# Attention of a two-layer trunk: stacked scores and a late block of heads, replaced by 64-row scores and heads spread over the projections

## The chip, the cores and the metric

The kernel runs on one core of a Trainium2 chip. The metric is the time of one execution on the device in microseconds, the median of several runs. The engines are named TensorE (PE; its weight loads are PEld), VectorE (DVE), ScalarE (ACT), GpSimd (POOL) and SyncE (SP, which here only issues DMAs).

## What is computed

A decoder trunk of two layers on one sequence of 256 tokens and 1024 features in float32. Layer 0 mixes tokens with attention, layer 1 with a matrix memory (mLSTM); a SwiGLU feed-forward network follows each, and a norm ends the trunk. The change touches layer 0's attention. With 256 tokens there is one key block of 256, so what remains of the block-sparse attention is plain causal softmax attention of 16 heads of 64:

```python
qkv = jnp.einsum('bsd,de->bse', xn, w_qkv).reshape(B, S, 3, ATTN_HEADS, ATTN_HEAD_DIM)
q = partial_rotary(qkv[0], cos, sin)
k = partial_rotary(qkv[1], cos, sin)
...
s_own = jnp.einsum('bhqd,bhkd->bhqk', qc, k_own, preferred_element_type=jnp.float32)
s_own = jnp.where(kpos[None, :] <= qpos[:, None], s_own, -jnp.inf)
p = jax.nn.softmax(jnp.concatenate([s_sel, s_own], axis=-1), axis=-1)
...
return jnp.einsum('bsd,de->bse', o, w_o)
```

## The kernel before

Activations lie transposed, features on partitions and tokens along a row. Every operand of a large matmul is split into a high and a low part (`xh`, `xl`, `wh`, `wl`; written `fp32r`), and `mm3` (L188) adds the three products high x high, high x low and low x high. Weights come as *units* of 128 x 1024 in the order of `unit_names` (L45): SP loads a unit into `raw` (L141), ScalarE casts it to `wh` (L159), VectorE subtracts for `wl` (L150). `prefetch` keeps four units of lead.

The attention stage runs in this order. `first_block` (L258) makes q and k of head pairs 0 to 3 in four PSUM banks, one unit per step of the contraction. Then a `Stream` (L293) walks through the rest: a generator per block of projections yields after every six matmuls of 256 columns (or three of 512), which is one *position*; work on heads hangs in a queue at positions, and a step that is not ready is tried again half a position later. The instructions of TensorE, VectorE and ScalarE keep the order in which they are recorded this way; GpSimd's and SP's come out of the scheduler. `ORDER` makes the stream v of heads 0 to 7, then q and k of pairs 4, 5, 6, part of v of heads 8 to 15, pair 7, the rest of v. Behind these come the output projection (`out_start`, `out_steps`) and `finish` (L375), then the feed-forward network.

A pair of heads goes through `rotary` (L480: a shuffle and a product on VectorE, a product and a sum on GpSimd), then `stacks` (L441): q and k are split into `u` (ScalarE cast L445, VectorE subtraction L449) and six DMAs (L452 to L454) put the parts of each head on top of each other in `stk`, so that one 128-row matmul does two of the three products:

```python
def dots(o, T, a0, na, m0, nm):
    a = T[:, 256 + a0:256 + a0 + na]
    mm(o, a, T[:, m0:m0 + nm], True, False)
    mm(o, a, T[:, 512 + m0:512 + m0 + nm], False, True)
```

A head then takes `scores` (L517), `softmax` (VectorE, L529), `exps` (ScalarE, L535), `recip`, `normalize` (ScalarE, L545), `transposes` (L555), the split of the transposed probabilities (`ph` on ScalarE L561, `pl` on VectorE L566) and `values` (L572). The heads start at position 26, one every 3 positions. v is kept as `VT` with the high and the low part of a head side by side in 128 columns, so the values of a head come out as two sums in 128 partitions; `heads_out` (ScalarE copy L591), `out_sum` (VectorE L597), `out_split` (L603) and `out_low` (L607) add the two, put two heads together and split the result for the output projection.

Of the kernel before, what the change touches and what calls it, by code (L numbers as in the profile page):

```python
# [24 lines left out]
ORDER = (0, 4, 5, 6, 1, 7, 1)  # L25
V1 = 4
# [18 lines left out]
def unit_names():  # L45
# [7 lines left out]
    def a_units():  # L53
        n, v = [], each("av", range(4))
        parts = {0: [v[0:4]], 1: [v[4:4 + V1 // 4], v[4 + V1 // 4:]]}
        for i in ORDER:
            n += parts[i].pop(0) if i < 4 else each("aqk", [i])
        return n

# [10 lines left out]
    n = outer("aqk") + a_units() + each("ao", range(4)) + ffn(0)  # L70
# [6 lines left out]
def trunk_kernel(ctx: ExitStack, tc: tile.TileContext, x, w, wg, fw, tab, out):  # L77
# [180 lines left out]
    def first_block(name, n, hooks={}):  # L258
# [164 lines left out]
    banks = first_block("aqk", n)  # L423
# [43 lines left out]
    with ExitStack() as actx:  # L467
# [10 lines left out]
        st = {}  # L478

        def rotary(hp, bank):  # L480
            b3 = bank.rearrange("p (g t) -> p g t", g=2)
            qk = ap.tile([P, 512], F32, name="qk", tag="qk", bufs=2)
# [12 lines left out]
        stacked = set()  # L495

        def v_evict(n0, banks, part=0):

            for t in range(2):
                dst = VT[:, t, n0 * 8:n0 * 8 + 8].rearrange("p (h two) d -> p h (two d)", two=2)  # L500
                hi = dst.rearrange("p h (c d) -> p h c d", d=64)[:, :, 0::3]
                src = banks[t].rearrange("p (h two d) -> p h two d", two=2, d=64)
                if part == 0:
                    nc.scalar.activation(hi, src, AF.Copy, scale=n.r[:, t:t + 1])
                    continue
                for o in range(2):
                    nc.vector.scalar_tensor_tensor(out=dst[:, :, 64 + o * 64:128 + o * 64], in0=src[:, :, o],  # L507
# [511 lines left out]
```

## Time and profile before

| what | value |
|---|---|
| median of 3 runs | 608.32 us (605.78 to 609.12) |
| profiled execution | 605.8 us |
| its span, first to last instruction | 604.0 us |
| mean granted TensorE clock | 0.996 |
| TensorE busy | 590.7 us (98%), 4524 matmuls |
| VectorE busy | 415.8 us (69%) |
| ScalarE busy | 340.9 us (56%) |
| GpSimd busy | 77.9 us (13%) |
| chain that ended last | PE 83%, DVE 5%, ACT 4%, DMA 3% |

Times in the profile count from the span's start. A timeline row has the start, the duration, the engine, the line, the operation, the tile it writes and those it reads, the size of the stationary tile, the size of the moving one, and in brackets the idle time before it with the engine whose work ended it. Matmuls overlap in the pipeline: what one costs is the distance between two starts, not its duration. A row of the chain has the start, the duration and the work that the end of the span hung on at that time. Names with a trailing `x48` stand for so many instructions.

### The profile page before, as it was taken

What the parts mean: (1) busy time and instruction counts of PE and PEld (TensorE: products, weight loads), DVE (VectorE), ACT (ScalarE), POOL (GpSimd) and SP (SyncE); (2) the same over time, 40 slices, a digit from 0 to 9 for tenths busy, and PEclk for the clock granted to TensorE, in tenths of its full rate; (3) what the DMA queues carried; (4) which work ended last, traced back from release to release, by engine and by line L of the source; (5) the groups of instructions that cost most, each with busy time, mean ns of one, the idle gap of its engine ahead of it and who ended that gap; (6) DMA issues with size and microseconds to landing.
All of it is one profiled execution on the core that took longest, in us unless ns stands there. A gap on an engine that the chain in (4) does not pass through costs nothing.

```text
span 604.0 us, 11573 instructions
## 1 busy us (share of the span) xinstructions
PE 590.7 (98%) x4524; PEld 561.2 (93%) x4524; DVE 415.8 (69%) x663; ACT 340.9 (56%) x611; POOL 77.9 (13%) x81
## 2 busy tenths in 40 slices
PE   8997999999999999999999999999999999999995
PEld 7987998999999999999999878999999999999984
DVE  5899898797866666566388678858776656556532
ACT  7645999767544444445275478846754444444412
POOL 2574320042000000000031300114100000000000
PEclk9999999999999999999999999999999999999999
DMA  8778965358655656555428868343955555565401
GB/s 312 286 216 260 263 200 159 140 180 305 214 196 189 207 179 206 183 201 190 163 81 302 255 218 222 110 141 117 308 175 200 178 187 197 175 194 190 141 0 69
DMA packets 36342, 116.39 MB, mean 193 GB/s; under 512 B 4544, under 2 KB 7360, under 8 KB 36288
## 3 DMA queue, kind: packets, MB, share of 16 engines
q1 hardware_dynamic: 36288, 115.66, 58.7%
q8 instruction: 35, 0.57, 0.4%
q14 instruction: 19, 0.16, 0.1%
HBM read 105.15 MB, written 1.05 MB: 176 GB/s over the span
## 4 chain that ended last, share of the span: by engine, by line
PE 83%; DVE 5%; ACT 4%; DMA 3%; issue 2%; SPq 1%; POOL 1%; POOLq 0%; ACTq 0%; DVEq 0%
PE ps L186 46%; PE acc L186 36%; DMA raw<-w 2%; DVE wl L150 2%; DMA stk<-u 1%; ACT wh L159 1%; ACT p L535 1%; ACT p L545 1%; DVE xl L207 1%; DVE u L449 1%; DVE VT L507 0%; PE ps L555 0%; SPq L452 0%; POOL sh L487 0%; POOL qk L488 0%
## 5 line engine op out<-in xcount | busy, mean ns | idle before, releaser
L150 DVE TENSOR_TENSOR wl<-raw,wh 128x1024 fp32r<-128x1024 f32 (+2 forms) x199 | 244.1, 1233 | 109.5 <-ACT wh L159 106.9
L159 ACT CAST wh<-raw 128x1024 fp32r<-128x1024 f32 (+2 forms) x199 | 205.5, 1038 | 184.9 <-PE ps L186 102.7
L186 PE MATMUL ps<-xh,wh 128*128 128x256 f32 x864 | 242.4, 281 | 0.8 <-ACT wh L159 0.8
L186 PE MATMUL ps<-xh,wl 128*128 128x256 f32 x864 | 241.0, 279 | 0.5 <-DVE wl L150 0.5
L186 PE MATMUL ps<-xl,wh 128*128 128x256 f32 x864 | 240.7, 279 | 0.0
L186 PEld LDWEIGHTS ps<-xh,wh 128*128 128x128 f32 x864 | 163.0, 189 | 2.1 <-ACT wh L159 1.2
L186 PEld LDWEIGHTS ps<-xh,wl 128*128 128x128 f32 x864 | 163.7, 189 | 1.1 <-DVE wl L150 1.1
L186 PEld LDWEIGHTS ps<-xl,wh 128*128 128x128 f32 x864 | 163.0, 189 | 0.7
L186 PE MATMUL acc<-hh,wh 128*128 128x256 f32 x176 | 48.6, 276 | 0.0
L186 PE MATMUL acc<-hl,wh 128*128 128x256 f32 x176 | 48.6, 276 | 0.0
L186 PE MATMUL acc<-hh,wl 128*128 128x256 f32 x176 | 48.6, 276 | 0.0
L219 POOL TENSOR_TENSOR ssum<-ssum,sq 128x512 f32<-128x512 f32 x12 | 20.5, 1708 | 198.6 <-issue 163.7
L644 DVE TENSOR_TENSOR tgu<-ps,R 128x512 f32<-128x512 f32 x42 | 28.6, 690 | 20.9 <-PE ps L186 20.9
L186 PE MATMUL acc<-wh,xh 128*128 128x512 f32 x96 | 39.0, 406 | 0.0
L186 PE MATMUL acc<-wh,xl 128*128 128x512 f32 x96 | 37.8, 393 | 0.0
L186 PE MATMUL acc<-wl,xh 128*128 128x512 f32 x96 | 37.7, 392 | 0.0
L186 PE MATMUL acc<-wh,hh 128*128 128x512 f32 x88 | 34.7, 394 | 0.0
L186 PE MATMUL acc<-wl,hh 128*128 128x512 f32 x88 | 34.7, 394 | 0.0
L186 PE MATMUL acc<-wh,hl 128*128 128x512 f32 x88 | 34.3, 390 | 0.0
L186 PEld LDWEIGHTS acc<-hl,wh 128*128 128x128 f32 x176 | 33.0, 188 | 0.0
L186 PEld LDWEIGHTS acc<-hh,wl 128*128 128x128 f32 x176 | 33.0, 188 | 0.0
L186 PEld LDWEIGHTS acc<-hh,wh 128*128 128x128 f32 x176 | 33.0, 188 | 0.0
(180 smaller groups left out, 853.8 us busy)
## 6 DMA issues: line engine op xcount, KB each, us to landing
raw<-w SPq DMA_DIRECT2D x195, 512.0 KB, 4.2
stk<-u SPq DMA_DIRECT2D x24, 192.0 KB, 4.3
stk<-u SPq DMA_DIRECT2D x24, 128.0 KB, 4.2
stk<-u SPq DMA_DIRECT2D x24, 64.0 KB, 3.6
out<-yout SPq DMA_DIRECT2D x4, 256.0 KB, 2.2
XV<-x SPq DMA_DIRECT2D x7, 128.0 KB, 6.2
tab_t<-tab SPq DMA_DIRECT2D x1, 708.0 KB, 6.9
fwb<-fw SPq DMA_DIRECT2D x1, 512.0 KB, 3.5
```

The source lines that it names most:

```text
L150: nc.vector.tensor_sub(wl[:, sl], raws[c][:, sl], wh[:, sl].bitcast(F32))
L159: nc.scalar.copy(wh[:, sl], raws[c][:, sl])
L186: nc.tensor.matmul(o, lhsT=lhsT, rhs=rhs, start=start, stop=stop, skip_group_check=True)
L207: nc.vector.scalar_tensor_tensor(out=self.l[:, f], in0=X[:, f], scalar=wc, in1=self.h[:, f].bitcast(F32), op0=ALU.mult, op1=ALU.subtract)
L219: nc.gpsimd.tensor_add(self.ssum, self.ssum, sq)
L449: nc.vector.tensor_sub(u[:, 512:1024], mv, u[:, 0:512].bitcast(F32))
L535: nc.scalar.activation(pt[:, sl], pt[:, sl], AF.Exp, bias=mx[:, t:t + 1], scale=-1.0, accum_out=ss[:, t:t + 1])
L545: nc.scalar.activation(pt[:, sl], pt[:, sl], AF.Copy, scale=ss[:, t:t + 1])
L644: nc.vector.tensor_mul(t.rearrange("p (g t) -> p g t", g=2), bank.rearrange("p (g t) -> p g t", g=2), n.R2())
```

## The change

- `first_block` of the attention (unit name `aqkv*`) makes q and k of pairs 0 and 1 and, in the two other banks, v of heads 0 to 7; the stream then makes q and k of pair 2, half of v of heads 8 to 15, pair 3, the other half, pairs 4 to 7. The number and the size of the units stay.
- `rotary` no longer leads to `stacks`. `split_qk` makes `u` (cast, and 1.5 positions later the subtraction), and `scores` multiplies straight from it: for each of two heads three products over the head's own 64 rows, the heads in turns, each into its own PSUM bank.
- Each pair of heads has a start of its own (`A_PAIR`), from position 9 to 73; its transposes follow 6 and 7 positions later, its values 12.
- `VT` keeps a head's high part in 64 columns and its low part in the next 64. `values` adds three products per half of the keys into 64 partitions, the two heads of a pair side by side along the row, so the sum of two halves is gone: `high_o` casts and `low_o` subtracts straight from PSUM.
- Buffers: `qk` 3, `u` 3, `p` 4, `ph` and `pl` 4, `oh` and `ol` 8.

```diff
-A_D1, A_X, A_D2, A_N, A_D3, A_L, A_D4, A_O1, A_O2 = 0.5, 1, 3, 1, 1, 1.5, 0.5, 1, 1
-A_O3, A_D5, A_D6, A_E, A_R, A_S, A_S2, A_W = 1, 2, 0, 1, 5, 6, 1.5, 1
-A_START, A_STEP, A_T, A_V = 26, 3.0, 8, 14
+A_PAIR = (9, 18, 27, 36, 48, 57, 65, 73)
+A_U, A_T, A_V, A_W = -4, 6, 12, 1
...
-    n = outer("aqk") + a_units() + each("ao", range(4)) + ffn(0)
+    n = outer("aqkv") + each("aqk", [2]) + each("av", [2]) + each("aqk", [3]) + each("av", [3])
+    n += each("aqk", range(4, 8)) + each("ao", range(4)) + ffn(0)
...
-            for i in range(4):
+            for i in range(pairs):
...
+            for t in range(4 - pairs):
+                mm3(banks[pairs + t], n.xt(k, t), (u[0][:, 512:1024], u[1][:, 512:1024]), k == 0, k == NF - 1)
...
-            def stack():
-                st[hp] = stacks(ap, qk, 3, later=lambda f: main.later(A_S2, lambda: (f(), stacked.add(hp))))
-            main.later(A_S, stack)
+            rq[hp] = qk
+
+        us = {}
+
+        def split_qk(hp):
+
+            qk = rq.pop(hp)
+            u = ap.tile([P, 1024], F32R, name="u", tag="u", bufs=3)
+            nc.scalar.copy(u[:, 0:512], qk)
+
+            def low_u():
+                nc.vector.tensor_sub(u[:, 512:1024], qk, u[:, 0:512].bitcast(F32))
+                us[hp] = u
+            main.later(1.5, low_u)
...
-        def scores(h):
-            T = st[h // 2][:, h % 2]
-            sc = ps_tile()
-            dots(sc[:, 0:P], T, 0, P, 0, P)
-            dots(sc[:, P:384], T, P, P, 0, S)
-            main.later(A_D1, softmax, h, sc)
+        def scores(hp):
+
+            u = us.pop(hp)
+            sc = [ps_tile() for _ in range(2)]
+            for o, a0, nm in ((0, 0, P), (P, P, S)):
+                for i, (al, ml) in enumerate(((0, 0), (0, 1), (1, 0))):
+                    for hh in range(2):
+                        r = slice(hh * 64, hh * 64 + 64)
+                        mm(sc[hh][:, o:o + nm], u[r, al * 512 + S + a0:al * 512 + S + a0 + P],
+                           u[r, ml * 512:ml * 512 + nm], i == 0, i == 2)
+            for hh in range(2):
+                main.later(0.5 + hh, softmax, 2 * hp + hh, sc[hh])
...
+            po = ps_tile()
             for hh in range(2):
-                r, q = slice(hh * 64, hh * 64 + 64), slice(64 - hh * 64, 128 - hh * 64)
-                nc.scalar.copy(o[r, :], po[q, hh * S:(hh + 1) * S])
-            main.later(A_O1, out_sum, hp, po, o)
...
+                p = pT.pop(2 * hp + hh)
+                for s, c, q in ((0, 0, 0), (1, S, P)):
+                    for i, (vl, pl) in enumerate(((0, 0), (0, 1), (1, 0))):
+                        mm(po[0:64, hh * S + q:hh * S + S], VT[:, s, 2 * hp + hh, vl * 64:vl * 64 + 64],
+                           p[pl][:, c:c + S - q], hh == 0 and s == 0 and i == 0, s == 1 and i == 2)
+            oh = ap.tile([P, S], F32R, name="oh", tag="oh", bufs=8)
+            ol = ap.tile([P, S], F32R, name="ol", tag="ol", bufs=8)
+            parts = [(slice(hh * 64, hh * 64 + 64), po[0:64, hh * S:hh * S + S]) for hh in range(2)]
+
+            def high_o():
+                for r, o in parts:
+                    nc.scalar.copy(oh[r], o)
+
+            def low_o():
+                for r, o in parts:
+                    nc.vector.tensor_sub(ol[r], o, oh[r].bitcast(F32))
+                ot[hp] = (oh, ol)
+            main.later(1, high_o)
+            main.later(2, low_o)
...
+        vb = tok_block("av", 2, n, lambda _, b: v_evict(1, b), lambda *a: main.later(0, *a))
+        main = Stream(*[(always, g) for g in (qk(2), islice(vb, 8), qk(3), vb, qk(4), qk(5), qk(6), qk(7))],
...
+        for hp in range(2):
+            main.at(0, rotary, hp, banks[hp])
+        main.at(0.5, v_evict, 0, banks[2:4])
+        for hp, s0 in enumerate(A_PAIR):
+            main.when(s0 + A_U, lambda hp=hp: hp in rq, split_qk, hp)
+            main.when(s0, lambda hp=hp: hp in us, scores, hp)
```

Three places show how the order moves. On GpSimd, at the start of the stream, `sh` is the shuffled copy that is multiplied by the sine and `qk` the sum (L487 and L488 before, L480 and L481 after); the number behind a name is its buffer. Before:

```order
L473 TENSOR_TENSOR Cr_462<-tab_t_109,R_411 128x256
L474 TENSOR_TENSOR Sr_463<-tab_t_109,R_411 128x256
L487 TENSOR_TENSOR sh_472<-sh_472,Sr_463 128x512
L488 TENSOR_TENSOR qk_471<-qk_471,sh_472 128x512
L487 TENSOR_TENSOR sh_506<-sh_506,Sr_463 128x512
L488 TENSOR_TENSOR qk_505<-qk_505,sh_506 128x512
```

After the change:

```order
L466 TENSOR_TENSOR Cr_414<-tab_t_109,R_369 128x256
L467 TENSOR_TENSOR Sr_415<-tab_t_109,R_369 128x256
L480 TENSOR_TENSOR sh_424<-sh_424,Sr_415 128x512
L480 TENSOR_TENSOR sh_430<-sh_430,Sr_415 128x512
L481 TENSOR_TENSOR qk_423<-qk_423,sh_424 128x512
L481 TENSOR_TENSOR qk_429<-qk_429,sh_430 128x512
```

The product of the second pair now stands ahead of the sum of the first.

On ScalarE, where heads 4 and 5 are normalised (`p<-p,ss`, L550 after the change), the second v eviction (`VT`, L505) falls between the two. After the change:

```order
L590 CAST oh_807<-ps_794 64x256 x2
L550 ACTIVATE p_772<-p_772,ss_771 128x128
L550 ACTIVATE p_772<-p_772,ss_771 128x256
L490 CAST u_823<-qk_736 128x512
L150 CAST wh_830<-raw_719 128x1024
L505 ACTIVATE VT_420<-acc_502,r_339 128x8x64
L505 ACTIVATE VT_420<-acc_503,r_339 128x8x64
L550 ACTIVATE p_786<-p_786,ss_785 128x128
L550 ACTIVATE p_786<-p_786,ss_785 128x256
```

Before, a cast of `u`, the exponentials of one head and two casts stood between the normalisations of two heads.

On TensorE, the values and scores (`ps<-stk`, `ps<-u`) of one place in the stream. Before, one head at a time, 128 rows:

```order
L186 MATMUL ps<-ph,VT 128x256
L186 MATMUL ps<-pl,VT 128x256
L186 MATMUL ps<-ph,VT 128x128
L186 MATMUL ps<-pl,VT 128x128
L555 MATMUL ps<-tab_t,p 128x128 x3
L186 MATMUL acc<-wh,xh 128x512
L186 MATMUL acc<-wl,xh 128x512
L186 MATMUL acc<-wh,xl 128x512
L186 MATMUL ps<-stk 128x128 x2
L186 MATMUL ps<-stk 128x256 x2
```

After the change, the first scores of the kernel, two heads in turns:

```order
L177 MATMUL acc<-wh,xh 128x512
L177 MATMUL acc<-wl,xh 128x512
L177 MATMUL acc<-wh,xl 128x512
L177 MATMUL ps<-u 128x128 x6
L177 MATMUL ps<-u 128x256 x6
L177 MATMUL acc<-wh,xh 128x512
L177 MATMUL acc<-wl,xh 128x512
L177 MATMUL acc<-wh,xl 128x512
```

They stand behind `qk(2)` and one position of v; between them and the transposes of their first head come 18 matmuls of 512 columns.

## Rows read from the trace of the kernel before

**Rows 1.** Windows: us, then busy time and count per engine, granted clock, DMA share, GB/s.

```profile
30.41:124.35 93.94, 89.42 (x660) 83.64 (x659) 82.85 (x187) 72.05 (x175) 27.39 (x17) 0.98 0.72 209
59.40:62.80 3.40, 3.40 (x15) 3.18 (x16) 2.11 (x8) 3.40 (x10) 1.84 (x2) 0.51 1.02 299
```

**Rows 2.** The chain that ended last, 60 to 158 us.

```profile
60.67 5.37 DMA stk<-u
...
70.29 0.88 ACT p L535 x4
...
71.58 0.36 ACT o L591
...
72.45 0.70 ACT p L545 x2
73.14 0.95 ACT wh L159
...
96.36 0.60 ACT VT L504
...
152.31 5.44 PE ps L186 x48
```

**Rows 3.** Timeline of TensorE, 68 to 71 us: scores, values, transposes.

```profile
68.31 0.62 PE L186 MATMUL ps<-stk 128*128 128x128 f32 x4
68.76 0.39 PE L186 MATMUL acc<-wh,xh 128*128 128x512 f32 x1
68.99 0.39 PE L186 MATMUL acc<-wl,xh 128*128 128x512 f32 x1
...
70.15 0.28 PE L186 MATMUL ps<-ph,VT 128*128 128x256 f32 x1
...
70.56 0.51 PE L555 MATMUL ps<-tab_t,p 128*128 128x128 f32 x3
70.83 0.48 PE L186 MATMUL acc<-wh,xh 128*128 128x512 f32 x1
```

**Rows 4.** Timeline of TensorE, 54 to 61 us.

```profile
54.74 0.69 PE L186 MATMUL ps<-stk 128*128 128x128 f32 x4 [1.26 <-issue]
...
59.40 1.09 PE L555 MATMUL ps<-tab_t,p 128*128 128x128 f32 x3 [2.44 <-ACT p L545]
...
60.49 0.41 PE L186 MATMUL ps<-xl,wh 128*128 128x256 f32 x1
60.71 0.41 PE L186 MATMUL ps<-xh,wl 128*128 128x256 f32 x1
```

**Rows 5.** Timeline of TensorE, 320 us: the last narrow matmul and the next.

```profile
320.45 0.28 PE L186 MATMUL acc<-xl,gws 128*32 128x256 f32 x1
320.56 0.28 PE L186 MATMUL ps<-xh,wh 128*128 128x256 f32 x1
```

**Rows 6.** Groups by line, whole span: output sums and casts.

```profile
L597 DVE TENSOR_TENSOR o<-ps,o 64x256 f32<-64x256 f32 x16 | 6.7, 420 | 3.5 <-ACT o L591 3.4
L603 ACT CAST oh<-o 128x256 fp32r<-128x256 f32 x8 | 3.2, 396 | 0.9 <-DVE o L597 0.9
```

**Rows 7.** Timeline of GpSimd, 35 us: a product beside little VectorE work.

```profile
35.23 1.30 POOL L487 TENSOR_TENSOR sh<-sh,Sr 128x512 f32<-128x512 f32 x1
```

**Rows 8.** The chain that ended last, 29 to 37 us.

```profile
29.35 0.73 DVE sh L485
...
30.79 2.25 POOL sh L487
...
33.12 2.17 POOL qk L488
...
35.31 0.63 ACT u L445
...
35.97 1.12 DVE u L449
```

**Rows 9.** Waits of TensorE from 63 to 93 us: total, times, longest.

```profile
PE ps L555 <- ACT wh L159: 0.2, 1, 0.2
```

More of the change, by code (lines that the diff above doesn't have):

```diff
@@ L24 @@
 A_LOOK = 4
-ORDER = (0, 4, 5, 6, 1, 7, 1)
-V1 = 4
 WBUFS = 8
@@ L51, in outer @@
         return [(name + "*", k, 0) for k in range(NF)]
[L53 to L58, printed above, removed]
     def ffn(l):
@@ L256, in pair_block, with first_block @@
             yield
-    def first_block(name, n, hooks={}):
+    def first_block(name, n, hooks={}, pairs=4):
         banks = [ps_tile() for _ in range(4)]
@@ L422, in trunk_kernel @@
     prefetch(NF - 1)
-    banks = first_block("aqk", n)
+    banks = first_block("aqkv", n, pairs=2)
     gw = const.tile([P, NF, 16], F32, name="gw")
@@ L494, in trunk_kernel, with v_evict @@
         evicted = set()
-        stacked = set()
-        def v_evict(n0, banks, part=0):
+        def v_evict(i, banks, part=0):
             for t in range(2):
-                dst = VT[:, t, n0 * 8:n0 * 8 + 8].rearrange("p (h two) d -> p h (two d)", two=2)
-                hi = dst.rearrange("p h (c d) -> p h c d", d=64)[:, :, 0::3]
-                src = banks[t].rearrange("p (h two d) -> p h two d", two=2, d=64)
+                dst = VT[:, t, i * 8:i * 8 + 8]
+                src = banks[t].rearrange("p (h d) -> p h d", d=64)
@@ L503, in v_evict @@
                 if part == 0:
[L504 to L507, printed above, removed]
-                                                   scalar=n.r[:, t:t + 1], in1=hi[:, :, o].bitcast(F32),
-                                                   op0=ALU.mult, op1=ALU.subtract)
+                    nc.scalar.activation(dst[:, :, 0:64], src, AF.Copy, scale=n.r[:, t:t + 1])
+                else:
+                    nc.vector.scalar_tensor_tensor(out=dst[:, :, 64:128], in0=src, scalar=n.r[:, t:t + 1],
+                                                   in1=dst[:, :, 0:64].bitcast(F32), op0=ALU.mult, op1=ALU.subtract)
@@ L510, in v_evict @@
             if part == 0:
-                main.later(A_E, v_evict, n0, banks, 1)
+                main.later(1, v_evict, i, banks, 1)
             else:
-                evicted.add(n0)
-        pr = {}
-        def scores(h):
-            T = st[h // 2][:, h % 2]
-            sc = ps_tile()
-            dots(sc[:, 0:P], T, 0, P, 0, P)
-            dots(sc[:, P:384], T, P, P, 0, S)
-            main.later(A_D1, softmax, h, sc)
+                evicted.add(i)
+        def scores(hp):
[9 more added lines that the diff above has]
+                main.later(0.5 + hh, softmax, 2 * hp + hh, sc[hh])
@@ L612, in qk @@
             yield from pair_block("aqk", hp, n, b)
-            main.later(A_D5, rotary, hp, b)
+            main.later(1, rotary, hp, b)
         acc = []
-        blocks = [tok_block("av", 2 * i, n, v_evict, lambda *a: main.later(A_D6, *a)) for i in range(2)]
-        parts = {0: [blocks[0]], 1: [islice(blocks[1], V1), blocks[1]]}
-        main = Stream(*[(always, parts[i].pop(0) if i < 4 else qk(i)) for i in ORDER],
+        vb = tok_block("av", 2, n, lambda _, b: v_evict(1, b), lambda *a: main.later(0, *a))
+        main = Stream(*[(always, g) for g in (qk(2), islice(vb, 8), qk(3), vb, qk(4), qk(5), qk(6), qk(7))],
                       ((lambda: 0 in ot and 1 in ot), out_start(acc, "ao", ot)), *[((lambda hp=hp: hp in ot), out_steps(acc, "ao", hp, ot)) for hp in range(2, 7)])
-        for hp in range(4):
-            main.at(A_R * hp, rotary, hp, banks[hp])
-        for h in range(16):
-            s0 = A_START + A_STEP * h
-            main.when(s0, lambda h=h: h // 2 in stacked, scores, h)
-            main.when(s0 + A_T, lambda h=h: h in pr, transposes, h)
-            main.when(s0 + A_V, lambda h=h: h in pT and h // 8 in evicted, values, h)
+        for hp in range(2):
[4 more added lines that the diff above has]
+            main.when(s0, lambda hp=hp: hp in us, scores, hp)
+            for hh in range(2):
+                main.when(s0 + A_T + hh, lambda h=2 * hp + hh: h in pr, transposes, 2 * hp + hh)
+            main.when(s0 + A_V, lambda hp=hp: 2 * hp in pT and 2 * hp + 1 in pT and hp // 4 in evicted, values, hp)
         with tc.manual_schedule(engines=vector_scalar):
@@ L965, in _chunks @@
     for n, i, h in unit_names():
-        if n.endswith("*"):
+        if n == "aqkv*":
+            r = wq[i * P:(i + 1) * P]
+            c = np.concatenate([r[:, c0:c0 + P] for c0 in (1024, 0, 1152, 128)] + [r[:, 2048:2560]], axis=1)
+        elif n.endswith("*"):
             a, ca, cb = pairs[n[:-1]]
```

58 lines of the change are left out of this document (15 added, 43 removed).

## Prediction

> **What bounds the kernel now.** I read first where TensorE spends the attention stage, and after that what it waits for. The first block of matmuls is over at 30.41 us and the first feed-forward block begins at 124.35 us; between them TensorE is busy 89.4 of 93.9 us, VectorE 82.9, ScalarE 72.1 [rows 1]. Busy time hides overlap, so I count work instead. A run of 48 matmuls of 256 columns takes 5.44 us [rows 2], 0.113 each; a weight unit is 24 of these, 2.72 us. The stage works off 24 units (16 for q, k and v, 8 for the output projection): 65.3 us. Per head there come scores (from 68.31 to 68.76: 0.45), values (70.15 to 70.56: 0.41) and three transposes (0.27) [rows 3], for 16 heads 18.1 us. Together 83.4 us of 93.9, so **10.5 us are lost**, and the change can win no more than that plus what it saves in matmuls.
>
> Of the loss, 1.26 us is a wait before the scores of the third head and 2.44 us one for the first normalised probabilities [rows 4]. Right behind them the granted clock is 0.51 for 3.40 us [rows 1], TensorE's lower level, and a matmul steps by 0.22 us instead of 0.113 [rows 4]: 1.6 us more. The other 5 us lie in small gaps. The cause of the two waits is the late start of the heads: q and k are copied by DMA into stacks (one such transfer takes 5.37 us on the chain [rows 2]), and the heads are then packed closely, so ScalarE sets the chain from 70 to 96 us with exponentials, normalisations, copies and weight casts in its own order [rows 2].
>
> **The change, part by part.** The sum is made against the profiled execution (605.8 us, span 604.0). That is the lowest of the three runs, 2.5 us under their median of 608.32, and I add the difference at the end.
>
> First block: two pairs of q and k and 512 columns of v instead of four pairs. Per unit 12 matmuls of 256 and 6 of 512 columns replace 24 of 256. The step of a 512-column matmul is 0.23 [rows 3], twice 0.113: zero. The DMA units keep their size and number: zero.
>
> Stacks: 48 DMAs go, with their place on SP's queue between the weight loads. Nothing else waits for them; what they cost is in the two waits above.
>
> Scores: per pair of heads 4 matmuls of 256 and 4 of 128 columns over 128 rows become 6 and 6 over 64 rows (one of 128 columns I count at half the step). No row shows a 64-row matmul. If the two heads run one after the other, a pair costs 6 x 0.113 + 6 x 0.057 = 1.02 us, plus 0.1 as before at the edge (0.90 now for two heads [rows 3]); if they run fully side by side 0.51. I take 0.70, since the heads alternate, use different rows and write different banks, so that nothing but issuing can hold them in line: 8 x (0.70 - 0.90) = **-1.6 us**, with ends at -3.1 and +1.6. The Trainium skill, "TensorE: Matmul & The Clock Gate", Part 3, has matmuls on different row groups run at the same time; by it alone the sum would be 1.5 us lower.
>
> Values: 4 matmuls per head become 6, on 64 columns of stationary data: 1.02 per pair instead of 0.82 [rows 3]. All write the same 64 partitions, so nothing runs side by side. With 0.08 for the edges 1.10: 8 x 0.28 = **+2.2 us**, ends +1.6 and +3.8. A narrow stationary operand costs no gap behind it: the first full-width matmul comes 0.11 us after the last one of 128*32 [rows 5], the normal step.
>
> Outputs: on ScalarE sixteen 64-row casts take the place of sixteen copies (0.36 each [rows 2]) and of eight 128-row casts (3.2 us [rows 6]); on VectorE sixteen 64-row subtractions that of sixteen 64-row sums (0.42 each [rows 6]) and of eight subtractions. So about 3 us less on each, on engines that are off the path except where a chain of one head is late. I price it at nothing by itself; it is the slack for the next item.
>
> Waits: the two old ones and the clock they cost go, -5.3 us; the heads are now spread 8 to 12 positions a pair, so ScalarE is no longer full. What is late next:
>
> (a) The first pair. TensorE makes qk(2) (48 matmuls, 5.44) and three of 512 columns from about 30.8, when VectorE has read the first bank, and is at the first scores at 36.9. GpSimd now multiplies both pairs before it adds the first, as the order shows: 30.79 + 2.25, then another multiplication (1.30 [rows 7] to 2.25), then the addition (2.17), 36.5 to 37.5; then ScalarE's cast 0.63 and VectorE's subtraction 1.12 [rows 8]: 38.3 to 39.2. A wait of 1.4 to 2.3; I take 1.5.
>
> (b) The first transposes. Behind the scores TensorE has 18 matmuls of 512 columns, 4.1 us. ScalarE needs for the first probabilities two heads of exponentials (0.88 each), a cast (0.95) and a normalisation (0.70) [rows 2], 3.4 us, and starts late, since VectorE first rotates the next pair (shuffle 0.73 [rows 8], and a product). About 1.2 us of waiting.
>
> (c) The fifth head. Between the normalisations of heads 4 and 5 ScalarE has a cast of u (0.63 [rows 8]), a weight cast (0.95) and the two v evictions (0.60 each); with the normalisation 3.5 us [rows 2]. TensorE has three transposes and six matmuls to cover it, 0.95 us. Up to 2.5; I take 1.8, since the first of the two is ready some time before it is asked for.
>
> (d) The other pairs: only u stands between two normalisations, 1.3 us against 0.95, and casts stand ahead of exponentials. Half a microsecond for each of six: 3.0. Behind every transpose the matmuls start late as they do now (in the 5 us of small gaps): 1.4.
>
> These make 8.9 us of loss where there are 10.5 now, **-1.6 us**. The sum is -1.6 + 2.2 - 1.6 = -1.0: 604.8 for a run like the profiled one, and **607.3 us** against the median. Everything behind 124.35 us is the same code and keeps its time. A measurement of this kernel can tell a change of about 0.5%, 3.0 us, from none; so I forecast no change.
>
> **Rivals.** *Faster: the slack swallows the new waits.* ScalarE would have 69 us of work and VectorE 79 in 93 us; if each engine runs ahead between pairs, (c) and (d) shrink from 4.8 to about 1, and scores at 0.65 add -0.4. That is 607.3 - 4.2 = 603.1 us. For it speaks that TensorE waits only 0.2 us between 63 and 93 us [rows 9], where ScalarE sets the chain [rows 2]; against it, that the order within each engine is fixed, so slack does not help a head that stands behind a cast.
>
> *Slower: the array is emptied at each change of shape.* The change puts 16 groups with 64 rows or 64 columns among full ones, 32 edges. A matmul of 256 columns is 0.28 long and steps by 0.11 [rows 5]; if at each edge the next had to wait for the end of the last, that is 0.17 x 32 = 5.4 us, hence 612.7. It decides from 0.13 us per edge upward. The rows speak against it: at the edge from 32 columns to 128 there is no gap [rows 5]; but none shows an edge in rows. The Trainium skill, "TensorEngine Tiling (Array Packing)", Key Properties, states the rule that changing the tiling mode drains TensorE. The trace does not agree with it where it can be seen, and so it gets a small chance.
>
> *Slower: ScalarE's order.* From scores to transposes TensorE has six positions of the stream (six matmuls of 0.113 each) and a pair's values, 5.2 us. The chain needs the reduction on VectorE, 1.76 of exponentials, perhaps a cast, the output casts of the pair before (0.72) and a normalisation, about 4.6. If at each of six pairs another cast stands in the way, each waits 1.0 more: 613.3. A clock that falls as it did after the old waits would add 1.6.
>
> *The heads do not run side by side:* 1.10 instead of 0.70 per pair, 3.2 us, 610.5: still no change by the bound.
>
> **How the numbers follow.** The forecast, with the last case, spans 605.3 to 611.3 and has 0.40. The faster case has 0.33: the two removed waits and the falling clock are certain gains, the new waits are not certain. The two slower ones have 0.12 and 0.15. The ends of the unknowns are scores -1.5 to +3.2, values -0.6 to +1.6, losses from 4 to 12 instead of 8.9; all on the good side give about 600, all on the bad side 615. Leaving out a tenth on either side, the range is 601.0 to 613.0; the likeliest case's own is 605.3 to 611.3.
>
> **What would show it.** In the profile after: no stk DMAs; the first 12 scores near 38 us after a wait of one to two; no stretch of lower clock near 60 us; a pair's scores in 0.6 to 0.8 us and its values in 1.1; a wait of the transposes of head 5 near 65 us; the feed-forward starting near 123 us. It is wrong if that start is before 120 or behind 127 us, or if a pair's scores or values take over 1.4 us.

## The result and the profile after

The changed kernel takes **610.83 us** by the median of 20 runs (609.80 to 612.14), the kernel before 607.74 in as many runs on the same chips (605.78 to 610.43). The ratio is 1.0053, with a 95% interval from 1.0042 to 1.0064: slower by 3.1 us, just over what this measurement tells from no change. No change was forecast, at 607.3; the range of 601 to 613 holds the time.

The profiled execution took 611.07 us with a span of 609.3 and a granted clock of 0.999; TensorE is busy 594.3 us with 4588 matmuls, VectorE 413.4, ScalarE 338.0, GpSimd 71.3. The execution profiled before was the lowest of its 20, the one after lies 0.24 over its median, so the traces differ by 5.3 us where the medians differ by 3.1.

The windows of the changed kernel (columns as in [rows 1]): the stage from the end of the first block to the feed-forward network, and the stretch that had the lower clock.

```profile
30.17:129.02 98.85, 92.97 (x769) 85.26 (x769) 80.99 (x176) 69.61 (x167) 23.16 (x17) 1.00 0.39 136
59.40:62.80 3.40, 3.40 (x24) 2.92 (x22) 2.11 (x8) 2.16 (x10) 0.00 (x0) 1.00 0.40 126
```

The stage grew from 93.9 us [rows 1] to 98.9. The stretch from 59.4 us has a granted clock of 1.00 in place of 0.51, the higher of TensorE's two levels. The chain has no stack DMA left. So the old waits and the low clock are gone as foreseen, and more came in their place. The first matmul of the feed-forward network starts at 129.02 us, and at 124.19 in the trace before; behind it 480.3 us are left, before 479.8.

TensorE's waits from 30 to 129 us (engine, line and tile that waited, who released it: us in total, times, longest):

```profile
PE ps L560 <- ACT p L550: 2.9, 3, 1.5
PE ps L177 <- DVE mx L532: 0.7, 1, 0.7
PE ps L177 <- DVE qk L479: 0.7, 1, 0.7
PE ps L177 <- DVE u L493: 0.7, 1, 0.7
PE ps L177 <- DVE pl L569: 0.5, 1, 0.5
```

Only the first row and the row of `u` are waits for data. TensorE's timeline at the places that the prediction named, and at those that it did not (L177 is `mm`, L560 the transposes):

```profile
31.01 0.36 PE L177 MATMUL ps<-xh,wh 128*128 128x256 f32 x1 [0.68 <-DVE qk L479]
...
63.51 0.49 PE L560 MATMUL ps<-tab_t,p 128*128 128x128 f32 x3
63.75 0.37 PE L177 MATMUL ps<-xh,wh 128*128 128x256 f32 x1
...
64.43 0.28 PE L177 MATMUL ps<-xh,wl 128*128 128x256 f32 x1
66.21 0.84 PE L560 MATMUL ps<-tab_t,p 128*128 128x128 f32 x3 [1.51 <-ACT p L550]
66.81 0.37 PE L177 MATMUL ps<-xh,wh 128*128 128x256 f32 x1
...
68.15 0.28 PE L177 MATMUL ps<-xh,wl 128*128 128x256 f32 x1
68.36 0.96 PE L177 MATMUL ps<-u 64*128 64x128 f32 x12
69.25 0.38 PE L177 MATMUL ps<-xh,wh 128*128 128x256 f32 x1
69.47 0.28 PE L177 MATMUL ps<-xl,wh 128*128 128x256 f32 x1
...
71.41 0.28 PE L177 MATMUL ps<-ph,VT 128*64 128x256 f32 x1
...
72.46 0.34 PE L177 MATMUL ps<-xh,wh 128*128 128x256 f32 x1
...
81.25 0.95 PE L177 MATMUL ps<-u 64*128 64x128 f32 x12
82.93 0.39 PE L177 MATMUL ps<-xh,wh 128*128 128x256 f32 x1 [0.73 <-DVE mx L532]
...
90.19 0.33 PE L177 MATMUL ps<-u 64*128 64x128 f32 x1
91.00 0.95 PE L177 MATMUL ps<-u 64*128 64x128 f32 x11 [0.48 <-DVE pl L569]
```

- Undisturbed, a pair's scores take 0.88 to 0.89 us from their first start to the next full matmul (68.36 to 69.25). They start 0.21 behind the last full matmul in place of 0.11 (68.15 to 68.36), and the first full matmul behind them steps by 0.22 in place of 0.11 (69.25 to 69.47). Over the normal steps a pair costs 0.88 + 0.09 + 0.11 = 1.08. Forecast was 0.70 with the edges. Before, two heads took 0.90 [rows 3], and the step behind them was the normal 0.23 of 512 columns.
- A pair's values take 1.05 (71.41 to 72.46); forecast 1.10.
- Head 5's transposes wait 1.51 at 66.21, the place that was named "near 65 us". Three transposes take 0.24 undisturbed (63.51 to 63.75) and 0.60 behind the wait.
- At 31.01, at 82.93 and within the scores at 91.00 TensorE waits for VectorE without using what VectorE makes.

The last point is read on VectorE. The rows at 82.23 and 82.58 are the softmax of the first head's two halves:

```profile
82.23 0.42 DVE L532 CUSTOM_DVE_ANT_0 p<-ps,tab_t 128x256 f32<-128x256 f32 x1 [1.09 <-PE ps L177]
82.58 0.29 DVE L532 CUSTOM_DVE_ANT_0 p<-ps,tab_t 128x128 f32<-128x128 f32 x1
...
89.26 1.22 DVE L141 TENSOR_TENSOR wl<-raw,wh 128x1024 fp32r<-128x1024 f32 x1
90.39 0.55 DVE L569 TENSOR_TENSOR pl<-ps,ph 128x384 fp32r<-128x384 f32 x1
```

At 82.93 the q,k block of pair 6 begins, and takes the PSUM bank whose scores VectorE has just read: the pool has four banks, and at that time the q,k block before it, the values of pair 3 and two scores stand in them. At 91.00 the second head's scores take the bank that VectorE still reads for `pl` (L569); that instruction stood behind a weight subtraction of 1.22. At 31.01 the bank is one of the first block, read by the rotation (L479).

### The profile page after: what moved, and what is told of

It reads as the page before. It is cut to its first block, busy times and chain, and to the rows that moved or that the text cites. A ratio compares the mean times of both kernels' runs of the same rounds, so it can differ in the third digit from the quotient of the medians.

```text
span 609.3 us, 11534 instructions
## 1 busy us (share of the span) xinstructions
PE 594.3 (98%) x4588; PEld 560.4 (92%) x4588; DVE 413.4 (68%) x651; ACT 338.0 (55%) x603; POOL 71.3 (12%) x81
## 3 DMA queue, kind: packets, MB, share of 16 engines
HBM read 105.15 MB, written 1.05 MB: 174 GB/s over the span
## 4 chain that ended last, share of the span: by engine, by line
PE 82%; DVE 6%; ACT 6%; DMA 2%; issue 1%; POOL 1%; SPq 0%; POOLq 0%; ACTq 0%
PE ps L177 45%; PE acc L177 36%; DVE wl L141 3%; ACT wh L150 2%; DMA raw<-w 2%; ACT p L550 1%; DVE p L532 1%; ACT xh L197 1%; DVE sh L478 1%; ACT p L538 1%; POOL ssum L210 1%; PE ps L560 1%; ACT sq L209 0%; ACT oh L590 0%; DVE qk L479 0%
## 5 line engine op out<-in xcount | busy, mean ns | idle before, releaser
L177 PE MATMUL ps<-xh,wh 128*128 128x256 f32 x864 | 243.0, 281 | 2.3 <-ACT wh L150 0.9
L177 PE MATMUL ps<-xh,wl 128*128 128x256 f32 x864 | 241.4, 279 | 0.7 <-DVE wl L141 0.7
L177 PE MATMUL ps<-xl,wh 128*128 128x256 f32 x864 | 240.8, 279 | 0.0
L177 PEld LDWEIGHTS ps<-xh,wh 128*128 128x128 f32 x864 | 162.5, 188 | 4.6 <-ACT wh L150 1.1
L177 PEld LDWEIGHTS ps<-xh,wl 128*128 128x128 f32 x864 | 163.4, 189 | 1.5 <-DVE wl L141 1.4
L177 PEld LDWEIGHTS ps<-xl,wh 128*128 128x128 f32 x864 | 162.4, 188 | 0.8
L177 PE MATMUL acc<-hl,wh 128*128 128x256 f32 x176 | 48.7, 277 | 0.0
L177 PE MATMUL acc<-hh,wh 128*128 128x256 f32 x176 | 48.7, 277 | 0.0
L177 PE MATMUL acc<-hh,wl 128*128 128x256 f32 x176 | 48.7, 277 | 0.0
L177 PE MATMUL acc<-wh,hh 128*128 128x512 f32 x88 | 34.7, 395 | 0.0
L177 PE MATMUL acc<-wl,hh 128*128 128x512 f32 x88 | 34.7, 394 | 0.0
L177 PE MATMUL acc<-wh,hl 128*128 128x512 f32 x88 | 34.4, 391 | 0.0
L177 PEld LDWEIGHTS acc<-hl,wh 128*128 128x128 f32 x176 | 33.1, 188 | 0.0
L177 PEld LDWEIGHTS acc<-hh,wl 128*128 128x128 f32 x176 | 33.0, 188 | 0.0
L177 PEld LDWEIGHTS acc<-hh,wh 128*128 128x128 f32 x176 | 33.0, 188 | 0.0
L177 PE MATMUL acc<-wh,xh 128*128 128x512 f32 x80 | 33.0, 412 | 0.0
L177 PE MATMUL acc<-wh,xl 128*128 128x512 f32 x80 | 31.6, 395 | 0.0
L177 PE MATMUL acc<-wl,xh 128*128 128x512 f32 x80 | 31.5, 394 | 0.0
```

Source lines behind the costliest of these rows:

```text
L177: nc.tensor.matmul(o, lhsT=lhsT, rhs=rhs, start=start, stop=stop, skip_group_check=True)
```

## The experiments

### What a pair's scores cost

Theory: six matmuls of 128 and six of 256 columns, two heads in turns, take about 0.7 us, and 0.3 is lost where TensorE goes from 128 rows to 64 and back. Rival: the heads don't overlap, so the twelve take 0.9 to 1.0 by themselves.

**e1: one head after the other.**

```diff
-            for o, a0, nm in ((0, 0, P), (P, P, S)):
-                for i, (al, ml) in enumerate(((0, 0), (0, 1), (1, 0))):
-                    for hh in range(2):
+            for hh in range(2):
+                for o, a0, nm in ((0, 0, P), (P, P, S)):
+                    for i, (al, ml) in enumerate(((0, 0), (0, 1), (1, 0))):
```

> Same matmuls as the change, but the scores of a pair are issued head by head instead of in turns. In the profile of the change the 12 score matmuls of a pair take 0.88 us from the first to the next other matmul, where 6 x 0.113 + 6 x 0.057 one after the other would be 1.02. If the two heads overlap because they alternate between the two halves of the rows, a pair now takes 1.02 or more: 8 x 0.14 = 1.1 us longer than the change. If nothing overlaps, the time stays within 0.3 us.

**e2: each score twice.**

```diff
-            for o, a0, nm in ((0, 0, P), (P, P, S)):
+            for o, a0, nm in ((0, 0, P), (P, P, S), (0, 0, P), (P, P, S)):
```

> The 12 score matmuls of each pair are issued twice (the second set writes the same result over the first). If the body of the scores costs what the profile shows (0.88 a pair, edges apart), the time grows by 8 x 0.88 = 7.0 us. If a good part of 0.88 is the edge at the change from 128 to 64 rows, it grows by less: 5.4 us where the edge is 0.2.

TensorE's timeline of the fourth pair in e1, and then in e2:

```profile
68.50 1.23 PE L177 MATMUL ps<-u 64*128 64x128 f32 x12
69.66 0.39 PE L177 MATMUL ps<-xh,wh 128*128 128x256 f32 x1
```

```profile
69.26 1.64 PE L177 MATMUL ps<-u 64*128 64x128 f32 x24
70.83 0.38 PE L177 MATMUL ps<-xh,wh 128*128 128x256 f32 x1
```

e1: 611.80 us (ratio 1.0067 [1.0046, 1.0089]; the interval overlaps that of the change, so the traces decide). In a row the twelve take 1.16, in turns 0.89.

The timeline merges the twelve; their single records show more. TensorE's timeline of the change, cut off at 68.40 us, has two of them under way:

```profile
68.36 0.33 PE L177 MATMUL ps<-u 64*128 64x128 f32 x2
```

In every turn of this group the two heads' matmuls start less than 0.01 us apart, so the heads run side by side in full. The turns start 0.16, 0.11, 0.11, 0.17 and 0.12 apart: those of 128 columns take as long as those of 256. In e1 the heads overlap too: the second begins 0.28 behind the first, at 68.78, with three matmuls of the first still to come. So e1 shows that turns are better than rows of six, and not what two heads cost without any overlap; the rival is out by the starts.

e2: 614.74 us (1.0113 [1.0092, 1.0134]). 24 matmuls take 1.57, so the second twelve cost 0.68 to 0.69, that is six turns of 0.11 to 0.12, and of the 0.88 of a group 0.19 is not the matmuls. The 0.70 of the prediction came out for the twelve alone, with no edge in it. The 3.9 us that e2 adds are less than 8 x 0.69 = 5.5, since part of them fills waits of the transposes.

**e9 and e10: one more change of rows.** A full-row matmul of 128 columns (bf16) is put ahead of the twelve (e9), or in their middle (e10, the `if o:`):

```diff
             for o, a0, nm in ((0, 0, P), (P, P, S)):
+                if o:
+                    nc.tensor.matmul(sc[0][:, 384:512], lhsT=warm[:, 0:P], rhs=warm[:, 0:P], start=True, stop=True,
+                                     skip_group_check=True)
```

> One matmul of 128 columns over all 128 rows (bf16, into unread columns of the first scores' bank) stands in front of each pair's twelve 64-row matmuls. It adds no change of rows. Edge theory (about 0.3 us are lost wherever TensorE goes from full rows to 64 rows and back: 0.09 on entry, 0.19 inside, 0.05 on leaving): a pair's group grows by the matmul's own 0.06 us, 8 x 0.06 = 0.5 us in the trace, 611.3 us by the median, the same as the change within the interval. Rival (the 0.3 us belong to the beginning of a group of scores whatever ran before: waits for u or for the bank): the same 0.06.

> The same extra matmul over 128 rows, now between the six 64-row matmuls of 128 columns and the six of 256, so that each pair goes from 64 rows to 128 and back once more; it waits for nothing. Edge theory: a pair's group grows from 0.88 to 0.88 + 0.06 + 0.33 = 1.27 us in the trace, 8 x 0.39 = 3.1 us; part of it fills waits of the transposes, so 612.5 to 613.9 us by the median. Rival (the 0.3 us are waits for u or a bank at the group's beginning): 0.94 us per pair, 611.3 us, the same as with the matmul in front.

TensorE's timeline of the eighth pair in e9, then in e10:

```profile
109.63 0.28 PE L177 MATMUL acc<-oh,wl 128*128 128x256 f32 x1
109.75 0.23 PE L518 MATMUL ps<-warm 128*128 128x128 bf16 x1
109.90 0.95 PE L177 MATMUL ps<-u 64*128 64x128 f32 x12
110.79 0.39 PE L177 MATMUL acc<-oh,wh 128*128 128x256 f32 x1
```

```profile
110.33 0.28 PE L177 MATMUL acc<-oh,wl 128*128 128x256 f32 x1
110.54 0.55 PE L177 MATMUL ps<-u 64*128 64x128 f32 x6
111.02 0.23 PE L520 MATMUL ps<-warm 128*128 128x128 bf16 x1
111.18 0.62 PE L177 MATMUL ps<-u 64*128 64x256 f32 x6
111.73 0.39 PE L177 MATMUL acc<-oh,wh 128*128 128x256 f32 x1
```

From the last full matmul ahead to the first behind it is 1.16 us in e9 (109.63 to 110.79) and 1.40 in e10 (110.33 to 111.73). The same instructions with two more changes of rows take 0.24 more: **0.12 us per change**. The other type shows no price on the way in: in e9 the step to the bf16 matmul is 0.12. The visit to 64 rows that every pair makes anyway loses more than its two changes at that price: 0.09 ahead of the scores, 0.19 inside and 0.11 behind, 0.39 in all. The times are 611.64 (1.0052 [1.0033, 1.0071]) and 612.42 (1.0073 [1.0045, 1.0101]); the second is just under what was expected, as 0.33 per round trip was too much. The rival, a loss at the beginning of a group whatever its rows, is out. The Trainium skill, "TensorEngine Tiling (Array Packing)", Key Properties, has a change of the tiling mode drain TensorE; for a change in rows the trace now agrees, at 0.12 us. For 64 columns it shows next to nothing: the twelve matmuls of the values take 1.05 where their steps make 1.02.

### Where the waits come from

**e5: the eviction of v's second half three positions later.**

```diff
-        vb = tok_block("av", 2, n, lambda _, b: v_evict(1, b), lambda *a: main.later(0, *a))
+        vb = tok_block("av", 2, n, lambda _, b: v_evict(1, b), lambda *a: main.later(3, *a))
```

> The second eviction of v comes three positions later, behind the normalisation of head 5. If the two evictions between the normalisations of heads 4 and 5 make the wait of 1.51 us at 64.4 us in the profile of the change, that wait shrinks to 0.4 or less and the time falls by 1.0 to 1.5 us against the change. If the chain of that head is late for another reason, the time stays within 0.3 us.

ScalarE's timeline between the normalisations (L550) of heads 4 and 5, in the changed kernel and then in e5:

```profile
62.45 0.80 ACT L550 ACTIVATE p<-p,ss 128x128 f32<-128x128 f32 x2
...
64.62 1.25 ACT L505 ACTIVATE VT<-acc,r 128x512 fp32r<-128x512 f32 x2
65.77 0.79 ACT L550 ACTIVATE p<-p,ss 128x128 f32<-128x128 f32 x2
```

```profile
64.83 0.80 ACT L550 ACTIVATE p<-p,ss 128x128 f32<-128x128 f32 x2
...
65.89 1.26 ACT L505 ACTIVATE VT<-acc,r 128x512 fp32r<-128x512 f32 x2
```

609.87 us (1.0040 [1.0026, 1.0054]), 1.0 less than the change, and head 5's transposes wait 0.38 in place of 1.51. The cause given under (c), evictions between two normalisations, is shown by the trace; the intervals of the two times overlap.

**e3: transposes and values one position later.**

```diff
-A_U, A_T, A_V, A_W = -4, 6, 12, 1
+A_U, A_T, A_V, A_W = -4, 7, 13, 1
```

> Transposes and values of each pair come one position later (7 and 13 instead of 6 and 12), that is 0.68 us more for the chain of softmax between them and the scores. If the waits of the transposes for the normalised probabilities are a matter of distance, as the theory says, most of the sixteen shrink by up to 0.68: 2 to 4 us less than the change. If ScalarE or VectorE simply cannot work faster, the waits move and the time stays within 0.7 us.

611.04 us (1.0053 [1.0034, 1.0072]): a miss, nothing by the time; the stage is 0.5 us shorter in the trace. The two largest groups of TensorE's waits from 30 to 129 us in e3:

```profile
PE ps L177 <- DVE qk L479: 3.6, 4, 1.1
PE ps L560 <- ACT p L550: 1.2, 2, 0.9
```

Waits for probabilities fall from 2.9 to 1.2 us, but four waits for L479 take 3.6 in place of 0.7. L479 rotates the next pair, which the waiting scores don't read: they wait for its bank. A later transpose keeps its bank later, and the scores are next in line. e12 below, which gives these q,k blocks other banks, leaves one of the four.

**e7: values of pairs 0 to 4 in the other pool's banks**, and **e11: q and k of pairs 2 to 6 there instead.**

```diff
-            po = ps_tile()
+            po = acc_tile() if hp < 5 else ps_tile()
```

```diff
-            b = ps_tile()
+            b = acc_tile() if hp < 7 else ps_tile()
             yield from pair_block("aqk", hp, n, b)
```

> The values of the first five pairs are written to banks of the other PSUM pool (idle there), so that the four banks of the pool with the scores serve one user less. If the scores of pairs 3 to 5 wait for a bank and not for data (their waits end with the reduction and the subtraction of other heads, at 81 and 90 us in the profile of the change), those 1.2 us go and the time falls by 1 us. If these waits are for the engines' work itself, they stay and the time is within 0.4 us.

> The sums of q and k of pairs 2 to 6 go into the four PSUM banks of the other pool, so that scores, transposes and values have their own pool of four to themselves. Theory (the scores of later pairs wait for a bank that an eviction on VectorE still reads): the waits of 0.73 us at 81 us, 0.48 at 90 us and the 0.68 at 30 us go or shrink to under 0.3 in all, and 1 to 1.9 us are won, 609.0 to 609.9 us. Rival (these waits only stand in front of those for ScalarE, which take their place): 610.3 to 611.3 us.

e7: 611.51 (1.0068 [1.0049, 1.0087]). e11: 611.78 (1.0070 [1.0048, 1.0092]). In e7 the wait at 81 us is gone, the one at 90 us stays at 0.48, and one of 0.33 for probabilities comes 5 us behind the first place; in e11 all three bank waits are gone, and the waits for probabilities grow from 2.9 to 3.7 us. So the banks are what those waits were for. In the trace of e11 the stage, from the transposes of the norm in the first block to the feed-forward, is 1.3 us shorter than in the changed kernel (29.05 to 129.59 against 27.14 to 129.02), as the theory expected, but the time does not show it: the first block itself ends 1.9 us later there. Up to 1.7 of that is the clock: in this execution it is 0.50 for 3.4 us from 10.87, ahead of the stage (the row is in the last section). e11's runs reach from 610.0 to 615.9, the four highest at a mean granted clock of 0.989 to 0.993; the three lowest, at 0.999, have 610.0 to 610.7, where six runs of the change at 0.999 have 610.0 to 611.5. The median of 611.78 lies above the rival's range too, so the time decides nothing here; what lowered the clock was not tried.

**e6: half of v's second block ahead of pair 2**, to cover the first rotation (the order of the weight units moves with it); **e4: pair 1's rotation three positions later**, so that GpSimd finishes pair 0 first; **e8: e3, e5, e6 and e7 together.**

```diff
-        main = Stream(*[(always, g) for g in (qk(2), islice(vb, 8), qk(3), vb, qk(4), qk(5), qk(6), qk(7))],
+        main = Stream(*[(always, g) for g in (islice(vb, 8), qk(2), qk(3), vb, qk(4), qk(5), qk(6), qk(7))],
```

```diff
-            main.at(0, rotary, hp, banks[hp])
+            main.at(3 * hp, rotary, hp, banks[hp])
```

> The stream begins with the first half of the second block of v (it writes two banks of the other pool) instead of q and k of pair 2. If TensorE's wait of 0.68 us at 30 us is for a PSUM bank that the rotation of the first pair still reads, it goes, and the time falls by 0.7 us. If q and k of pair 2 now come late for their own rotation, scores of pair 2 wait and the time rises.

> The rotation of the second pair comes three positions later, so GpSimd adds the first pair before it multiplies the second. If the order on GpSimd makes the wait of 0.66 us before the first scores, the scores come 0.7 to 1.5 us earlier and the time falls by 0.7 to 1.0 us against the change. If something else is late there (the banks, VectorE), nothing moves: within 0.3 us.

> The three edits above together, and transposes and values one position later. If PSUM banks and order make the waits, one position more now pays where it did not alone (same time in the third experiment, because the waits moved from the transposes to the scores): 4 to 6 us less than the change, hence 1 to 3 us less than the kernel before. If ScalarE and VectorE are the bound, the time stays within 1.5 us of the change.

e6: 610.84 (1.0054 [1.0039, 1.0069]): the bank wait at 30 us goes, the first scores wait 1.72 for `u` in place of 0.66, and the second scores 0.87 for a bank. The wait of the first transposes goes. e4: 612.56 (1.0080 [1.0056, 1.0104]), a miss: the first scores no longer wait, but the first transposes wait 1.84 in place of 1.00, since TensorE leaves the first scores 1.4 us earlier, at 37.85, and the first normalisation starts only 0.6 earlier, at 43.64. Behind that wait the granted clock is 0.50 for 3.4 us from 45.2, which costs up to 1.7 of the trace's stage. e8: 610.94 (1.0054 [1.0038, 1.0070]), another miss by the time, with a stage 1.4 us shorter in the trace: the transposes' waits go, the first scores wait 1.43 for `u`, and later ones five times, 0.8 to 1.1 each, for L479 or L569.

### Both kinds of wait together

**e12** is e3, e5 and e11 in one. **e13** also starts the first three pairs later; **e14** is e13 with the last q,k block in the other banks too; **e15** is e13 with `u` at its old positions; **e16** is e15 with three later pairs moved.

```diff
-A_PAIR = (9, 18, 27, 36, 48, 57, 65, 73)
+A_PAIR = (12, 20, 28, 36, 48, 57, 65, 73)
...
-            main.when(s0 + A_U, lambda hp=hp: hp in rq, split_qk, hp)
+            main.when((5, 14, 23)[hp] if hp < 3 else s0 + A_U, lambda hp=hp: hp in rq, split_qk, hp)
```

(The first pair of lines is e13 to e15, the second e15 and e16; e14 has `acc_tile()` for every pair, e16 `A_PAIR` with 37, 48, 57, 66, 75 at its end.)

> The other banks for q and k, the second eviction of v three positions later, and transposes and values one position later. Theory (the losses are the two kinds of wait together, for PSUM banks by the scores and for normalised probabilities by the transposes; where each was removed alone the other grew): both are small at last, the waits behind 45 us under 1.5 us in all, and the time is 606.5 to 608.5 us, within 0.3% of the kernel before. Rival (the chain of a pair through VectorE and ScalarE is as long as the distance, so a wait comes back elsewhere): 609.5 to 611 us.

> As e12_banks_vt_t7, with the first three pairs' scores at positions 12, 20 and 28 in place of 9, 18 and 27, so that TensorE has three more positions of projections (2.1 us) while the first pair's u is made. Theory (the first pair's 1.6 us of waiting are lost for want of other work, not passed on): the wait before the first scores is under 0.3, no wait of over 0.5 appears at the next two pairs, 1.0 to 1.6 us less than e12: 607.1 to 607.8 us. Rival (the second pair's chain, then only eight positions behind, waits in its place): within 0.5 us of e12's 608.7.

> As e13_first_pair_later, with the last q,k block too in the other pool's banks. Theory (the 1.2 us that the scores at 96 us wait behind the product of the last pair are for the bank that this block holds): that wait goes, and unless the output projection's start waits for its four banks instead, 0.8 to 1.2 us less than e13: 606.0 to 607.0 us, at or a little under the kernel before (607.5). Rival (the wait moves to the output projection, whose four banks are then one short): the same as e13 within 0.5.

> As e13_first_pair_later, but the steps that make u of the first three pairs keep their old positions 5, 14 and 23. In e13 they had moved with the scores, and VectorE's subtraction for u then stood behind a weight subtraction and the rotation of the next pair. Theory (order on VectorE): the first scores, at about 38.4 us, wait under 0.4 us, as u is ready near 38.4 us; 2.0 us less than e13 in the trace of this stage, 606.6 to 607.6 us by the median. Rival (the wait returns elsewhere): 608.2 to 608.9 us.

> As e15_later_u_early, with the scores of pairs 3, 6 and 7 one, one and two positions later (37, 66, 75). Theory (the 1.2 us at 95 us are a wait for the bank of the last q,k block, which one position, 0.69 us, covers in part): that wait shrinks to 0.5 and the time is 0.5 to 0.7 us less than e15. Rival (the later last pair delays the end of the heads in front of the output projection by its two positions): the same as e15 or up to 0.7 us more.

| run | stage in the trace, us | of it at clock 0.50 | median us | ratio to before |
|---|---|---|---|---|
| before | 96.75 | 3.4 | 607.74 | |
| the change | 101.88 | none | 610.83 | 1.0053 [1.0042, 1.0064] |
| e12 | 98.06 | none | 608.73 | 1.0008 [0.9994, 1.0022] |
| e13 | 97.33 | none | 608.65 | 1.0003 [0.9987, 1.0020] |
| e14 | 99.26 | 6.8 | 608.74 | 1.0004 [0.9987, 1.0021] |
| e15 | 97.43 | 3.4 | 607.51 | 0.9985 [0.9971, 1.0000] |
| e16 | 100.14 | 6.8 | 607.90 | 0.9996 [0.9981, 1.0012] |

(The stage counts from the start of the transposes of the norm in the first block to that of the first matmul of the feed-forward.)

The stages can't be compared as they stand. At 0.50 a matmul steps by 0.22 in place of 0.113 [rows 4], so such a stretch costs up to half its length. Without it the stage of e15 would be about 95.7, an estimate: 1.6 less than e13's, near the 2.0 that its theory expected.

e12 takes back 2.1 of the 3.1 us, where its parts alone gave 1.0 (e5) or nothing by the time (e3, e11). In the traces its stage is 3.8 us shorter than that of the change, and the three parts make 1.2 (e5), 0.5 (e3) and 1.3 (e11): a little more together than alone. That fits the two kinds of wait standing behind each other, but rests on one trace of each. The medians show less than the stages; the runs of e12 to e16 have a mean granted clock of 0.991 to 0.999, those of the change 0.994 to 0.999. Its 608.73 is 0.2 over what the theory expected. TensorE's waits from 30 to 129 us, in e12 and then in e15:

```profile
PE ps L177 <- DVE u L493: 1.6, 1, 1.6
PE ps L177 <- DVE qk L479: 1.2, 1, 1.2
PE ps L560 <- ACT p L550: 1.2, 2, 0.9
```

```profile
PE ps L560 <- ACT p L550: 1.4, 1, 1.4
PE ps L177 <- DVE qk L479: 1.2, 1, 1.2
...
```

e13 was to take away the first wait of e12; it grew to 2.4. VectorE's timeline of e13 shows why: `u`'s subtraction (L493) had moved with the scores, behind a second weight subtraction and the next pair's rotation.

```profile
34.07 4.49 DVE L141 TENSOR_TENSOR wl<-raw,wh 128x1024 fp32r<-128x1024 f32 x2
...
39.70 1.40 DVE L493 TENSOR_TENSOR u<-qk,u 128x512 fp32r<-128x512 f32 x1
```

With `u` back in its place (e15) that wait is gone and one of 1.4 for the first probabilities is back; the time is 607.51, as its theory expected, 3.3 us below the change and level with the kernel before, at the edge of the interval. Its stage is still 0.7 us longer than before, with as long a stretch at 0.50 in either. e14 and e16 add nothing by the median, two misses: in e14 the last bank wait goes, and the values of a pair wait 0.97 for `pl` instead; in e16 it stays at 1.23. No version ran that is clearly faster than the kernel before.

## Why the prediction was wrong

The sum came to 604.8 for the profiled execution, which took 611.07: 6.3 too little. Within the stage, us in all (measured: what groups and edges take over normal steps, and for waits each group's time over its undisturbed time):

| step | forecast | measured |
|---|---|---|
| scores of eight pairs, with their edges | 5.6 | 8.6 (8 x 1.08) |
| values, with their edges | 8.8 | 8.8 (8 x 1.05, 0.4 behind) |
| (a) first pair's `u` | 1.5 | 0.9 |
| (b) to (d) waits for probabilities | 6.0 | 5.9 |
| waits for PSUM banks | none | 2.5 |
| late start behind transposes | 1.4 | 1.5 |

These make 4.9 of the 6.3; 0.5 lies behind the stage (480.3 for 479.8), the rest is not assigned. So two steps failed: the cost of the scores, 3.0 too low, and the PSUM banks, which the sum did not have.

- **Scores: failed.** "I take 0.70, since the heads alternate" was to hold the edges, and the change was to win 1.6 us here. A pair takes 1.08: 0.69 for the twelve (e2) and 0.39 for the visit to 64 rows (e9 and e10 show that changes of rows cost). Two heads cost 0.90 before, so the scores lost about 1.4 us. That the twelve alone came to 0.69 is luck. The prediction put them between no overlap (1.02) and full overlap (0.51). The overlap is full, but a matmul of 128 columns does not cost "half the step". [rows 3] had shown that: its two of 128 and two of 256 columns take 0.45, four steps of 0.11.
- **Rival "the heads do not run side by side": right in time, wrong in mechanism.** Its 1.10 per pair and 610.5 us are near what was measured (1.08, 610.83), but the heads do run side by side, and its sum has no bank wait.
- **Rival "emptied at each change of shape": true in rows, not in columns.** Its price of 0.17 x 32 = 5.4 us was too high: the visits to 64 rows cost 8 x 0.39 = 3.1. It was dismissed by a row that shows a change in columns only [rows 5].
- **Values: right**, 1.05 and 0.06 behind, where 1.10 was forecast.
- **(a) to (c): right in place and about right in size**: first scores at 37.53 with a wait of 0.66, first transposes 1.00, head 5 at 66.21 with 1.51. e5 confirms the cause of (c).
- **"Behind every transpose the matmuls start late ... 1.4": right.** Behind each of the sixteen groups of transposes the first two steps are together 0.09 over the normal ones, 1.5 us in all. The like behind and ahead of the scores had no term; it is in their 1.08.
- **PSUM banks: not seen.** Before, two heads' scores came into the pool one bank at a time; now two are asked for at once, out of four. The prediction let qk(2) start when "VectorE has read the first bank" and left that wait out of the sum. Three of them cost 2.5 us in the trace, and e11, which moves the q,k blocks, is without all three. e3 and e8 show that they also take up what is won elsewhere.
- **Low clock: right.** No stretch near 60 us is below 1.00.
- **The step to the median: off.** 2.5 us were added because the execution profiled before lay that far below its median. The one after lies at its median, so of 6.3 us only 3.5 remain as the miss (610.83 for 607.3).

## What to carry to other kernels

Ahead of a change that doubles what is asked of a pool at once, list who holds each PSUM bank when the next one is asked for; a wait taken from one user of a full pool comes back at the next, so test fixes for banks and for data together. Cost matmuls of another number of rows with their edges, here 0.39 us for a visit from 128 to 64 rows and back, and take the step of a short matmul from the trace and not from its columns: here 128 columns cost as much as 256 in the scores. When work is moved later, look at what its inputs' steps are then recorded behind.

## What was unexpected on the chip

Two heads of 64 rows run at the same time, and a pair still costs more than two stacked heads did, 1.08 against 0.90. Six turns of 0.11 to 0.12 make 0.69, where full overlap by the columns would make 0.51, and the visit to 64 rows takes 0.39. The weight loads of successive turns start 0.11 to 0.12 apart as well, so they may set the turn; no run shows it. The Trainium skill, "TensorE: Matmul & The Clock Gate", Part 3, has such matmuls run at the same time; the trace agrees, with starts less than 0.01 us apart.

VectorE and GpSimd slow each other down, and which of the two depends on the work. In the timeline of the changed kernel the weight subtraction takes 2.24 us at 34.53, beside GpSimd's sums (34.41 to 37.92), and 1.21 at 38.39 behind them; the subtraction of `u` 1.77 at 36.69, and 0.69 later. The prediction took 1.12 for it. Beside a product of GpSimd the weight subtraction takes only 1.27 (32.02), and there it is the product that takes 2.29 in place of 1.31. The Trainium skill, "GPSIMD Engine Reference", 1. Specifications, has the SBUF interfaces shared, with contention where a VectorE instruction has two SBUF inputs, which these have; the trace agrees beside the sums.

A wait of one to three microseconds may or may not be followed by the low clock. In e13 a wait of 2.4 us before the first scores leaves it at 1.00; in e14, one of 2.7 at the same place is followed by 0.50, and in e16 one of 1.8 before the first transposes. In e12 and e15 the scores of pair 6 wait 1.23, and only e15's clock falls behind it. Stretches (columns as in [rows 1]) of e13, e16, e15 and e11:

```profile
42.00:44.00 2.00, 2.00 (x9) 1.66 (x10) 2.00 (x6) 0.31 (x1) 0.23 (x1) 1.00 0.00 0
```

```profile
48.00:50.00 2.00, 2.00 (x16) 1.67 (x14) 0.00 (x0) 1.22 (x2) 0.00 (x0) 0.50 0.82 256
```

```profile
97.10:100.51 3.41, 3.41 (x18) 3.41 (x18) 2.79 (x9) 2.18 (x10) 0.40 (x1) 0.50 0.29 62
```

```profile
10.87:14.28 3.41, 3.41 (x14) 3.11 (x14) 3.08 (x4) 3.41 (x6) 1.39 (x1) 0.50 1.04 416
```

Runs of one kernel differ with it: of e15's twelve, the three from 605.1 to 605.7 us have a mean granted clock of 0.998 or 0.999, the two of 608.7 one of 0.992 and 0.994. What decides between the two was not tried.
